# Attention scores in plain fp32 in two row tiles of TensorE, in a hybrid Hyena, Conformer and memory-attention encoder

## The chip, the cores and the metric

The kernel runs on one core of a Trainium2 chip. A core has a matrix engine (TensorE, PE in the profile; its weight loads are PEld), three engines for elementwise work (VectorE or DVE, ScalarE or ACT, GpSimd or POOL), a queue engine (SyncE or SP), and 16 DMA engines. Each engine works through its own instructions in order; they wait for each other through semaphores. TensorE writes its results to PSUM, from where VectorE and ScalarE read them. The metric is the device time of one execution in microseconds (us).

## The reference

Two request groups, each a sequence of 2048 positions with 1024 channels and a memory of 256 tokens, go through the same encoder layer. One projection `h @ w_in` of the normalised input feeds three branches: a Hyena branch (a short convolution, a long convolution by FFT, gates), a Conformer branch (gated, a convolution of 31 taps, LayerNorm), and attention with 4 heads of 64 channels into the memory tokens. The branches are gated, joined, projected by `w_out`, added to the input and normalised. All of it is fp32. What the change touches is this:

```python
def memory_attention(q, mem_n, w_kv):
    k, v = jnp.split(mem_n @ w_kv, 2, axis=-1)
    q = q.reshape(B, L, N_XHEADS, HEAD_DIM)
    k = k.reshape(B, M, N_XHEADS, HEAD_DIM)
    v = v.reshape(B, M, N_XHEADS, HEAD_DIM)
    s = jnp.einsum('blhd,bmhd->bhlm', q, k).astype(jnp.float32) * (HEAD_DIM ** -0.5)
    p = jax.nn.softmax(s, axis=-1).astype(v.dtype)
    o = jnp.einsum('bhlm,bmhd->blhd', p, v)
    return o.reshape(B, L, D_XATTN)
```

## The kernel before

**Stages.** The projection stage normalises x, splits it into a high and a low part (`xh`, `xl`, a type that TensorE multiplies at reduced precision, F32R) and computes 26 columns of 128 channels for each of the two request groups (L426 to L428: high times high, low times high, high times low, over 8 slices of 1024 channels). Each column runs over 4 blocks of 512 tokens; the result of each stands in a PSUM tile `pj` (2 buffers), and a small function for the kind of column reads it out. Between the blocks a background queue is worked off in steps: keys and values of the memory, the Conformer branch, the Hyena filter, the first of the Hyena FFT. The last columns of group 0 are worked together with the loading, normalising and splitting of the next group's x. The attention stage handles 16 blocks of 512 queries of a pair of heads (`attention`), and between them 24 first-stage FFT steps of the Hyena branch (`stage_a`, two to a block as long as there are any; the transposes of L178 and the matmuls of L185 are theirs). The stage after it does the rest of the long convolution (`stage_b`), the last stage the inverse transform, `w_out` and the final norm.

**Order.** The kernel is written in a tile framework that plans the order of each engine's instructions by its own simulation of the time line, and puts in the semaphores. So the order on an engine is not that of the code: the scores of the next half block run ahead of Hyena steps written before them. A tile that is reused waits for its last reader.

**Queries.** `xa_q` scales the projection by 0.125 and splits it: ScalarE writes the high part (L533), VectorE the rest (L534). Both read `pj`. Four DMAs on SP (L537) store the parts to `QS` in DRAM, so that 64 rows hold the high and 64 the low part of a head. `queries` loads a block, 512 KB, on GpSimd's queue (L733), one block ahead.

**Keys.** `kv_background` transposes the keys and writes them four heads wide with the high part in both halves of the partitions and the low part beside zeros (L586 to L589), and stores them to `KB`. `load_kv` loads them for the attention stage (L722).

**Scores.** With high and low parts stacked over the 128 rows, a score tile of 128 queries by 256 memory tokens is two matmuls over all 128 rows (L757): the stacked query parts against the high keys twice over, and against the low keys with zeros. For each half block `u` of 256 queries and each tile `t` of 128, both heads stand in one PSUM tile `sc` (`ms`, 2 buffers). VectorE takes the negated maximum (L761), ScalarE the exponential with its sum (L765), VectorE the reciprocal, GpSimd the product (L769). TensorE transposes the four parts (L772), ScalarE or VectorE copies them out (L774), and after both `t` plain fp32 matmuls multiply them with the values (L779), the two heads in the two halves of the array's columns.

**Places.** The attention stage's SBUF tiles lie where x lay before: `woh[0:4]` under the high x tile of token block 0, `wol[0:4]` under that of block 2. Keys, values and queries use such places, since `w_out` comes into them only later: keys and values of group 0 in `woh[0]`, `woh[1]` and `woh[3]`, those of group 1 in `wol[0:3]`, queries in `woh[2]` and `wol[5]` in turn.

Of the kernel before, what the change touches and what calls it, by code (L numbers as in the profile page):

```python
# [18 lines left out]
P = 128  # L19
L = 2048  # L20
# [82 lines left out]
def kernel(ctx: ExitStack, tc: tile.TileContext, a: dict):  # L103
# [11 lines left out]
    QS = [[dram.tile([2, 64, 2, L], F32R, name=f"qs{g}{c}") for c in range(2)] for g in range(2)]  # L115
    ZX = [[dram.tile([P, L], F32, name=f"zx{g}{c}") for c in range(2)] for g in range(2)]
    KB = [dram.tile([P, 2048], F32R, name=f"kb{g}") for g in range(2)]
# [81 lines left out]
    with ExitStack() as c1:  # L199
# [10 lines left out]
        def sm(n=TB, dt=F32):  # L210
            return smp.tile([P, n], dt, tag="sm", name=nm("sm"))
# [318 lines left out]
        def xa_q(g, i):  # L530
            def f(tb, ps):
                qh, ql = sm(TB, F32R), sm(TB, F32R)
                nc.scalar.activation(qh, ps, AF.Copy, scale=0.125)  # L533
                nc.vector.scalar_tensor_tensor(ql, ps, 0.125, qh.bitcast(F32), op0=ALU.mult, op1=ALU.subtract)  # L534
                for j, q in enumerate((qh, ql)):
                    for h in range(2):
                        nc.sync.dma_start(QS[g][i][j, :, h, tb * TB:(tb + 1) * TB].bitcast(F32),  # L537
                                          q[64 * h:64 * h + 64, :].bitcast(F32))
            return (COL_Q + i * P, f)

        def kv_background():
# [24 lines left out]
            def store(g):  # L566
# [13 lines left out]
                kt = big(2048, F32R)  # L580
                kb = kt.rearrange("p (h q m) -> p h q m", h=4, q=2)
                for h in range(4):
                    r = slice(64 * (h % 2), 64 * (h % 2) + 64)
                    ro = slice(64 - 64 * (h % 2), 128 - 64 * (h % 2))
                    src = pk[r, (h // 2) * 256:(h // 2 + 1) * 256]
                    nc.scalar.copy(kb[r, h, 0, :], src)  # L586
                    nc.scalar.copy(kb[ro, h, 0, :], src)
                    nc.vector.tensor_tensor(kb[0:64, h, 1, :], src, kb[r, h, 0, :].bitcast(F32), op=ALU.subtract)
                    nc.gpsimd.memset(kb[64:128, h, 1, :].bitcast(F32), 0.0)  # L589
                nc.sync.dma_start(KB[g].bitcast(F32), kt.bitcast(F32))  # L590

# [112 lines left out]
    with ExitStack() as c2:  # L704
# [14 lines left out]
        def load_kv(g):  # L719
            kt, vt = ((woh[0:2], woh[3]), (wol[0:2], wol[2]))[g]  # L720
            for i in range(2):
                nc.gpsimd.dma_start(kt[i], KB[g][:, i * 1024:(i + 1) * 1024])  # L722
            vt = vt.bitcast(F32)[:, 0:512]
# [284 lines left out]
```

## Time and profile before

| | |
|---|---|
| median of three runs | 2121.18 us (2119.74 to 2125.28) |
| the profiled execution, its own time | 2124.94 us |
| its span, first to last instruction | 2123.2 us |
| TensorE matmuls busy | 1993.2 us, 94% |
| VectorE, GpSimd, ScalarE busy | 1267.3, 895.0, 758.1 us |

The profile is of one execution. A row of a group gives line, engine, operation, out<-in, the shapes, and how many there are; "idle before" is the time in which the engine stood still in front of it, and what ended that. A matmul's duration holds the time that its results need through the array, so matmuls that follow each other overlap; what one costs in a stream is read from the distance of the starts.

### The profile page before, as it was taken

How to read it: one execution, taken by the hardware profiler on the slowest of the kernel's cores; microseconds unless marked ns; L12 is line 12 of the kernel's file. 1: busy time of each engine (PE TensorE's matmuls, PEld its weight loads, DVE VectorE, ACT ScalarE, POOL GpSimd, SP SyncE). 2: the span in 40 equal slices, each digit the busy share in tenths (PEclk: the TensorE clock that was granted, in tenths of full speed). 3: DMA queues.
4: the chain of work that ended last, by engine and by line, in shares of the span. 5: the costliest groups of instructions: out<-in, count | busy, mean ns of one | idle time of the engine just before them, and what ended most of it. 6: DMA issues, size and time to landing. Idle time of an engine off the chain costs nothing.

```text
span 2123.2 us, 26265 instructions
## 1 busy us (share of the span) xinstructions
PE 1993.2 (94%) x9058; PEld 1552.7 (73%) x9058; DVE 1267.3 (60%) x1747; ACT 758.1 (36%) x1439; POOL 895.0 (42%) x854
## 2 busy tenths in 40 slices
PE   5999988898999999999999899999988899999998
PEld 5888877786877788786777777767433378888886
DVE  5756397978326364469595963278787533444443
ACT  5531212131424233231333244278687611112111
POOL 3423476655533111455554541266598611111111
PEclk9999999999999999999999999999999999999999
DMA  9643333332656422222322236688888685565552
GB/s 337 207 150 134 95 90 100 110 110 79 213 194 219 129 106 100 75 91 81 90 87 107 80 111 207 224 275 264 238 273 271 215 197 153 145 152 145 153 149 55
DMA packets 238557, 329.71 MB, mean 155 GB/s; under 512 B 87177, under 2 KB 117913, under 8 KB 236634
## 3 DMA queue, kind: packets, MB, share of 16 engines
q1 hardware_dynamic: 146026, 261.70, 39.3%
q10 hardware_dynamic: 87056, 54.57, 9.2%
q0 software_dynamic: 5344, 11.77, 2.0%
q8 instruction: 72, 1.18, 0.2%
q14 instruction: 59, 0.48, 0.1%
HBM read 197.35 MB, written 130.61 MB: 154 GB/s over the span
## 4 chain that ended last, share of the span: by engine, by line
PE 58%; DVE 18%; DMA 8%; POOL 6%; issue 5%; ACT 4%; SPq 1%; ACTq 0%; POOLq 0%; DVEq 0%
DVE bg L230 11%; PE pj L427 10%; PE pj L426 10%; PE pj L428 10%; PE ms L953 5%; PE ms L955 5%; PE ms L954 5%; PE tr L936 2%; DMA bg<-in_x_sample_dram 2%; DMA in<-x1d 2%; DVE sm L449 2%; PE tr L772 1%; PE po L779 1%; PE ms L757 1%; PE ms L564 1%
## 5 line engine op out<-in xcount | busy, mean ns | idle before, releaser
L426 PE MATMUL pj<-xh,whi 128*128 128x512 f32 (+1 forms) x1728 | 671.5, 389 | 30.7 <-ACT sm L440 8.4
L427 PE MATMUL pj<-xl,whi 128*128 128x512 f32 (+1 forms) x1728 | 670.2, 388 | 7.4 <-POOL xl L397 5.1
L428 PE MATMUL pj<-xh,wlo 128*128 128x512 f32 (+1 forms) x1728 | 668.8, 387 | 0.3 <-DMA wlo<-ws 0.3
L230 DVE SCALAR_TENSOR_TENSOR bg<-bg,vb,bg 128x512 f32<-128x512 f32 x480 | 419.7, 906 | 12.9 <-POOL bg L225 8.0
L426 PEld LDWEIGHTS pj<-xh,whi 128*128 128x128 f32 x1728 | 331.7, 192 | 101.5 <-ACT sm L440 10.4
L427 PEld LDWEIGHTS pj<-xl,whi 128*128 128x128 f32 x1728 | 332.2, 192 | 72.5 <-POOL xl L397 6.2
L428 PEld LDWEIGHTS pj<-xh,wlo 128*128 128x128 f32 x1728 | 331.9, 192 | 64.9 <-DMA wlo<-ws 0.8
L953 PE MATMUL ms<-wo,mh 128*128 128x512 f32 x512 | 207.0, 404 | 2.0 <-ACT mh L188 2.0
L954 PE MATMUL ms<-wo,mh 128*128 128x512 f32 x512 | 201.5, 394 | 0.0
L955 PE MATMUL ms<-wo,ml 128*128 128x512 f32 x512 | 198.8, 395 | 0.0
L447 POOL TENSOR_SCALAR sm<-sm,va 128x448 f32<-128x448 f32 (+1 forms) x96 | 121.2, 1263 | 159.2 <-ACT sm L440 152.9
L449 DVE SCALAR_TENSOR_TENSOR sm<-sm,va,sm 128x448 f32<-128x448 f32 (+1 forms) x96 | 83.9, 874 | 153.4 <-POOL sm L447 122.8
L956 DVE TENSOR_TENSOR xr<-xr,ms 128x512 f32<-128x512 f32 x64 | 44.0, 687 | 203.4 <-PE ms L955 202.4
L468 POOL TENSOR_TENSOR big<-big,sm 128x448 f32<-128x448 f32 (+1 forms) x64 | 120.2, 1878 | 102.8 <-DVE sm L451 99.4
L195 POOL TENSOR_TENSOR ss<-ss,mhalf 128x1 f32<-128x1 f32 x32 | 17.7, 552 | 315.8 <-DVE ss L194 315.8
L193 ACT ACTIVATE junk<-xr 128x1024 bf16<-128x1024 f32 x32 | 33.8, 1057 | 318.4 <-DVE xr L956 318.4
L440 ACT COPY sm<-pj 128x512 f32<-128x512 f32 x96 | 56.1, 585 | 220.3 <-PE pj L428 186.9
L953 PEld LDWEIGHTS ms<-wo,mh 128*128 128x128 f32 x512 | 97.4, 190 | 20.8 <-ACT mh L188 2.8
L955 PEld LDWEIGHTS ms<-wo,ml 128*128 128x128 f32 x512 | 96.4, 188 | 20.8 <-POOL ml L189 0.3
L954 PEld LDWEIGHTS ms<-wo,mh 128*128 128x128 f32 x512 | 97.4, 190 | 19.2
L189 POOL TENSOR_TENSOR wlo<-sm,whi 128x512 fp32r<-128x512 f32 x50 | 79.7, 1608 | 63.4 <-ACT whi L188 47.3
L827 POOL TENSOR_TENSOR z<-z,us 128x512 f32<-128x512 f32 x64 | 81.5, 1283 | 33.9 <-DVE us L826 26.2
(171 smaller groups left out, 2877.7 us busy)
## 6 DMA issues: line engine op xcount, KB each, us to landing
big<-in_xt_dram SPq DMA_DIRECT2D x32, 512.0 KB, 5.5
in<-x1d SPq DMA_DIRECT2D x128, 128.0 KB, 3.8
aa<-o ACTq DMA_DIRECT2D x64, 256.0 KB, 4.1
at<-aa SPq DMA_DIRECT2D x64, 256.0 KB, 3.9
out_dram<-xr ACTq DMA_DIRECT2D x64, 256.0 KB, 3.4
sm<-in_win_dram SPq DMA_DIRECT2D x52, 256.0 KB, 3.2
ws<-whi SPq DMA_DIRECT2D x52, 256.0 KB, 2.2
ws<-wlo SPq DMA_DIRECT2D x52, 256.0 KB, 4.0
```

Of the source, the lines that this page charges most:

```text
L189: (sub_eng or nc.gpsimd).tensor_tensor(lo, src, hi.bitcast(F32), op=ALU.subtract)
L230: nc.vector.scalar_tensor_tensor(st["a", c], st["h", c][:, k:k + TB], vb[:, 2 * k + c:2 * k + c + 1], st["a", c], op0=ALU.mult, op1=ALU.add)
L426: nc.tensor.matmul(ps[:, ts_], hi, xh[:, k, ts_], start=k == 0, stop=False)
L427: nc.tensor.matmul(ps[:, ts_], hi, xl[:, k, ts_], start=False, stop=False)
L428: nc.tensor.matmul(ps[:, ts_], lo, xh[:, k, ts_], start=False, stop=k == KC - 1)
L447: nc.gpsimd.tensor_scalar(ct[:, o:e], pt[:, o + 1:e + 1], w[1], va[:, 52 + ch:53 + ch], op0=ALU.mult, op1=ALU.add)
L449: nc.vector.scalar_tensor_tensor(ct[:, o:e], pt[:, o:e], w[0], ct[:, o:e], op0=ALU.mult, op1=ALU.add)
L468: nc.gpsimd.tensor_tensor(v, v, out, op=ALU.mult)
L827: nc.gpsimd.tensor_tensor(z, z, us, op=op)
L953: nc.tensor.matmul(po, mh[:, k, :], woh[k][:, hs], start=i == 0, stop=False)
L954: nc.tensor.matmul(po, mh[:, k, :], wol[k][:, hs], start=False, stop=False)
L955: nc.tensor.matmul(po, ml[:, k, :], woh[k][:, hs], start=False, stop=i == 7)
```

## The change

Queries and keys are no longer split. `xa_q` is one ScalarE copy and one store. The keys are stored as they come from the transposes, with the two heads of a pair on rows 0 to 63 and 64 to 127. A score tile is one plain fp32 matmul over 64 rows, and the two heads' matmuls lie in the upper and the lower half of the array's rows (row tiles). They write two PSUM tiles: `sc[h]` holds a head with both `t` side by side, instead of a `t` with both heads. Maximum, exponentials, reciprocal and product are then done for each head, and the transposes of a `t` come after both heads' products. Keys and values of group 0 now lie in `woh[0]` and `woh[1]`, those of group 1 in `woh[2]` and `woh[3]`, and queries in `wol[0]` and `wol[1]` in turn.

```diff
     HD = [[dram.tile([P, L + 2 * CH], F32, name=f"hd{g}{c}") for c in range(2)] for g in range(2)]
     SZ = [[dram.tile([P, L], F32, name=f"sz{g}{c}") for c in range(2)] for g in range(2)]
-    QS = [[dram.tile([2, 64, 2, L], F32R, name=f"qs{g}{c}") for c in range(2)] for g in range(2)]
+    QS = [[dram.tile([P, L], F32, name=f"qs{g}{c}") for c in range(2)] for g in range(2)]
     ZX = [[dram.tile([P, L], F32, name=f"zx{g}{c}") for c in range(2)] for g in range(2)]
-    KB = [dram.tile([P, 2048], F32R, name=f"kb{g}") for g in range(2)]
+    KB = [dram.tile([P, 512], F32, name=f"kb{g}") for g in range(2)]
...
         def xa_q(g, i):
             def f(tb, ps):
-                qh, ql = sm(TB, F32R), sm(TB, F32R)
-                nc.scalar.activation(qh, ps, AF.Copy, scale=0.125)
-                nc.vector.scalar_tensor_tensor(ql, ps, 0.125, qh.bitcast(F32), op0=ALU.mult, op1=ALU.subtract)
-                for j, q in enumerate((qh, ql)):
-                    for h in range(2):
-                        nc.sync.dma_start(QS[g][i][j, :, h, tb * TB:(tb + 1) * TB].bitcast(F32),
-                                          q[64 * h:64 * h + 64, :].bitcast(F32))
+                q = sm()
+                nc.scalar.activation(q, ps, AF.Copy, scale=0.125)
+                nc.sync.dma_start(QS[g][i][:, tb * TB:(tb + 1) * TB], q)
...
                         nc.tensor.transpose(pk[:, i * 256 + s * P:i * 256 + (s + 1) * P],
                                             kv[:, s * 256 + i * P:s * 256 + (i + 1) * P], ident)
-                kt = big(2048, F32R)
-                kb = kt.rearrange("p (h q m) -> p h q m", h=4, q=2)
-                for h in range(4):
-                    r = slice(64 * (h % 2), 64 * (h % 2) + 64)
-                    ro = slice(64 - 64 * (h % 2), 128 - 64 * (h % 2))
-                    src = pk[r, (h // 2) * 256:(h // 2 + 1) * 256]
-                    nc.scalar.copy(kb[r, h, 0, :], src)
-                    nc.scalar.copy(kb[ro, h, 0, :], src)
-                    nc.vector.tensor_tensor(kb[0:64, h, 1, :], src, kb[r, h, 0, :].bitcast(F32), op=ALU.subtract)
-                    nc.gpsimd.memset(kb[64:128, h, 1, :].bitcast(F32), 0.0)
-                nc.sync.dma_start(KB[g].bitcast(F32), kt.bitcast(F32))
+                kt = bt()
+                nc.scalar.copy(kt, pk)
+                nc.sync.dma_start(KB[g], kt)
...
 
         def load_kv(g):
-            kt, vt = ((woh[0:2], woh[3]), (wol[0:2], wol[2]))[g]
-            for i in range(2):
-                nc.gpsimd.dma_start(kt[i], KB[g][:, i * 1024:(i + 1) * 1024])
-            vt = vt.bitcast(F32)[:, 0:512]
+            kt, vt = (t.bitcast(F32)[:, 0:512] for t in (woh[2 * g], woh[2 * g + 1]))
+            nc.gpsimd.dma_start(kt, KB[g])
             nc.gpsimd.dma_start(vt, VT[g])
-            kvs[g] = ([t.rearrange("p (h q m) -> p h q m", h=2, q=2) for t in kt],
-                      vt.rearrange("p (i m c) -> p i m c", i=2, m=2))
+            kvs[g] = (kt.rearrange("p (i m) -> p i m", i=2), vt.rearrange("p (i m c) -> p i m c", i=2, m=2))
 
         qn = [0]
 
         def queries(g, i, tb):
-            qt = (woh[2], wol[5])[qn[0] % 2]
+            qt = wol[qn[0] % 2].bitcast(F32)[:, 0:TB]
             qn[0] += 1
-            nc.gpsimd.dma_start(qt.rearrange("p (h t) -> p h t", h=2),
-                                QS[g][i][:, :, :, tb * TB:(tb + 1) * TB].rearrange("q r h t -> (q r) h t"))
+            nc.gpsimd.dma_start(qt, QS[g][i][:, tb * TB:(tb + 1) * TB])
...
                 pt = pts[pn[0] % 6]
                 pn[0] += 1
+
+                sc = ms(), ms()
                 for t in range(2):
-                    sc = ms()
                     for h in range(2):
-                        q0 = h * TB + u * 256 + t * P
-                        for j in range(2):
-                            nc.tensor.matmul(sc[:, h * 256:(h + 1) * 256], qt[:, q0:q0 + P], kb[i][:, h, j, :],
-                                             start=j == 0, stop=j == 1)
+                        r, q0 = slice(64 * h, 64 * h + 64), u * 256 + t * P
+                        nc.tensor.matmul(sc[h][:, t * 256:(t + 1) * 256], qt[r, q0:q0 + P], kb[r, i, :],
+                                         start=True, stop=True)
+                e = []
+                for h in range(2):
                     mx = tiny.tile([P, 2], F32, tag="mx", name=nm("mx"))
                     se = tiny.tile([P, 2], F32, tag="se", name=nm("se"))
-                    nc.vector.tensor_reduce(mx, sc.rearrange("p (h m) -> p h m", h=2), axis=AX.X, op=ALU.max,
+                    nc.vector.tensor_reduce(mx, sc[h].rearrange("p (t m) -> p t m", t=2), axis=AX.X, op=ALU.max,
                                             negate=True)
-                    e = eps_[2 * u + t]
-                    for h in range(2):
-                        nc.scalar.activation(e[:, h * 256:(h + 1) * 256], sc[:, h * 256:(h + 1) * 256], AF.Exp,
-                                             bias=mx[:, h:h + 1], accum_out=se[:, h:h + 1])
+                    e.append(eps_[2 * u + h])
+                    for t in range(2):
+                        nc.scalar.activation(e[h][:, t * 256:(t + 1) * 256], sc[h][:, t * 256:(t + 1) * 256], AF.Exp,
+                                             bias=mx[:, t:t + 1], accum_out=se[:, t:t + 1])
                     nc.vector.reciprocal(se, se)
-                    ev = e.rearrange("p (h m) -> p h m", h=2)
+                    ev = e[h].rearrange("p (t m) -> p t m", t=2)
                     nc.gpsimd.tensor_tensor(ev, ev, se.unsqueeze(2).broadcast_to([P, 2, 256]), op=ALU.mult)
+                for t in range(2):
                     tp = tr()
                     for k in range(4):
-                        nc.tensor.transpose(tp[:, k * P:(k + 1) * P], e[:, k * P:(k + 1) * P], ident)
-                    tv = tp.rearrange("p (k t) -> p k t", k=4)
-                    (nc.vector.tensor_copy if t else nc.scalar.copy)(pt[:, :, t * P:(t + 1) * P], tv)
+                        nc.tensor.transpose(tp[:, k * P:(k + 1) * P],
+                                            e[k // 2][:, t * 256 + k % 2 * P:t * 256 + (k % 2 + 1) * P], ident)
+                    (nc.vector.tensor_copy if t else nc.scalar.copy)(
+                        pt[:, :, t * P:(t + 1) * P], tp.rearrange("p (k t) -> p k t", k=4))
```

## Rows read from the trace of the kernel before

**Rows 1.** The page: the span, and a group of part 5 (columns as explained above).
```profile
span 2123.2 us, 26265 instructions
...
L426 PE MATMUL pj<-xh,whi 128*128 128x512 f32 (+1 forms) x1728 | 671.5, 389 | 30.7 <-ACT sm L440 8.4
```
**Rows 2.** Busy time by stretch (window, length, busy us of each engine, clock, DMA, GB/s).
```profile
100.00:160.00 60.00, 60.00 (x267) 49.17 (x266) 38.76 (x66) 22.07 (x49) 17.12 (x20) 1.00 0.41 147
```
**Rows 3.** Waits of PE, 594 to 705 us (total us, times, longest).
```profile
PE pj L426 <- DVE sm L534: 5.8, 5, 2.0
```
**Rows 4.** Timeline around one of these waits (start us, length us).
```profile
645.37 0.59 ACT L533 ACTIVATE sm<-pj 128x512 fp32r<-128x512 f32 x1
...
648.95 0.50 PE L426 MATMUL pj<-xh,whi 128*128 128x512 f32 x1 [1.08 <-DVE sm L534]
```
**Rows 5.** Busy time by stretch, attention stage (order PE, PEld, DVE, ACT, POOL).
```profile
1438.00:1458.00 20.00, 20.00 (x157) 14.62 (x154) 15.89 (x33) 16.61 (x54) 13.43 (x17) 1.00 0.91 288
```
**Rows 6.** Timeline of PE over one block of the attention stage.
```profile
1443.73 1.20 PE L757 MATMUL ms<-wo,wo 128*128 128x256 f32 x8
...
1448.20 1.20 PE L757 MATMUL ms<-wo,wo 128*128 128x256 f32 x8
1449.24 0.60 PE L178 MATMUL tr<-ident,u 128*128 128x128 f32 x4
1449.77 1.08 PE L779 MATMUL po<-ynp,wo 128*64 128x256 f32 x8
1450.79 0.66 PE L772 MATMUL tr<-ident,ynp 128*128 128x128 f32 x4
1451.38 0.50 PE L185 MATMUL pa<-k,th 64*128 64x512 f32 x2
1451.71 0.40 PE L185 MATMUL pa<-k,tl 64*128 64x512 f32 x2
1451.95 0.39 PE L185 MATMUL pa<-k,th 64*128 64x512 f32 x2
1452.27 0.66 PE L772 MATMUL tr<-ident,ynp 128*128 128x128 f32 x4
1452.68 1.20 PE L757 MATMUL ms<-wo,wo 128*128 128x256 f32 x8
1453.81 0.51 PE L185 MATMUL pa<-k,th 64*128 64x512 f32 x2
```
**Rows 7.** Timeline of GpSimd's queue at the end of the projection stage.
```profile
1354.57 0.73 POOL L733 DMA_DIRECT2D wo<-qs  x1
...
1363.73 1.08 POOL L722 DMA_DIRECT2D wo<-kb  x2 [4.72 <-PE pj L428]
```
**Rows 8.** The query loads of L733, all 16: from issue to landing.
```profile
DMA to landing us min/median/max: 4.2/5.7/9.2
```
**Rows 9.** Timeline at the start of the attention stage.
```profile
1368.70 0.63 PE L757 MATMUL ms<-wo,wo 128*128 128x256 f32 x4
...
1370.14 0.68 DVE L761 TENSOR_REDUCE mx<-ms 128x2 f32<-128x512 f32 x1
...
1370.85 0.47 ACT L765 ACTIVATE ynp<-ms,mx 128x256 f32<-128x256 f32 x1
```
**Rows 10.** Three lines' matmuls (records, ns min/median/max, first and last start).
```profile
L757 PE MATMUL ms<-wo,wo x256: 274/283/682, 1368.7 to 1514.1; 128*128 128x256 f32 x128
...
L820 PE MATMUL tr<-in,stab x128: 592/592/1061, 1505.5 to 1685.2; 128*128 128x512 f32 x128
...
L779 PE MATMUL po<-ynp,wo x256: 379/379/431, 1380.7 to 1524.5; 128*64 128x256 f32 x128
```
**Rows 11.** Timeline of ACT: the last accumulator read of a half block.
```profile
1451.94 0.22 ACT L765 ACTIVATION_READ_ACCUMULATOR ynp<-ms,mx 128x1 f32 x1
```
**Rows 12.** Timeline of PE where no Hyena step is left.
```profile
1496.92 1.08 PE L779 MATMUL po<-ynp,wo 128*64 128x256 f32 x8
...
1500.65 1.08 PE L779 MATMUL po<-ynp,wo 128*64 128x256 f32 x8
```

## The prediction

> **What bounds the kernel now.** I read the page first, then the busy times by stage, then for each stage the waits of TensorE and the timeline. The profiled execution spans 2123.2 us [rows 1]. The change touches three places: the query and key steps of the projection stage (0 to 1368 us), the start of the attention stage (1368 to 1378 us), and the attention stage itself (to about 1526 us).
>
> In the projection stage TensorE is nearly always busy; where the keys are stored (137 to 149 us) it is busy in every microsecond [rows 2]. So work on ScalarE, VectorE and GpSimd counts here only where TensorE waits for it. The list of waits has one such place: in the last chunks of the first request group, TensorE waits five times, 5.8 us together, for the subtraction of L534 [rows 3]. One of the five shows why: ScalarE has read the projection out by 645.96 us (645.37 + 0.59), but the PSUM tile comes free only after VectorE, which is deep in the normalisation of the second group, has done its half as well; the next projection starts at 648.95 us, 1.08 us late [rows 4].
>
> In the attention stage TensorE is busy 20.00 of 20 us, the other engines at most 17 [rows 5]. TensorE's timeline there is a row of groups without gaps; the score group that stands in front of L185 returns from 1443.73 to 1452.68 us, so a block takes 8.95 us and half a block (256 queries, one score group) 4.48 us [rows 6]. What this stage is worth is therefore read from TensorE's order of groups, and from whether a new wait enters it.
>
> **The change, part by part.**
>
> *Queries.* It removes 16 subtractions on VectorE and 48 of 64 stores on SP. Ten of the subtractions hide behind TensorE and are worth nothing, the last belongs to the start of the attention stage below, and the five above are worth at most 5.8 us. With ScalarE alone reading, the tile of rows 4 is free 2.25 us before TensorE is. Behind the wait I find nothing that comes due at once except the casts of the next x tiles, which follow TensorE on ScalarE's queue and so move with it. I take 5.0 us of gain, bounds 0 (the order of the stage's instructions is planned anew, and another wait takes the place) and 5.8.
>
> *Keys.* 16 casts, 8 subtractions and 8 memsets become 2 copies. All lie under the full 60 us of TensorE in rows 2: nothing, and were the cover gone, a gain.
>
> *Start of attention.* The first queries go from a place that lay under the x tile of the first token block to one under the third block's (the two are freed in the order in which the last projections end). Before, the load was issued at 1354.57 us; now it can't be before about 1363.73 us, where the second group's keys, which lay under that same tile, got their release [rows 7]. GpSimd's queue behind it (second queries, second keys, the first u block) waited for that release in any case. Landing takes 4.2 to 9.2 us, median 5.7 [rows 8], so the queries are there at 1369.4 us (1367.9 to 1372.9), against first scores at 1368.70. But the first exponential starts only at 1370.85 us [rows 9]; scores from 1369.4, a group of 1.1 us (below) and a reduction of 0.68 [rows 9] make 1371.2. The last subtraction, which held up the first reduction until 1370.14, is gone, but the exponential waits no longer for that than for the scores. I take +0.5 us, bounds -0.5 and +3.
>
> *Score matmuls.* First the streaming. A split matmul of 512 columns takes 389 ns [rows 1], one of 256 columns 283 [rows 10]: 106 ns per 256 columns. Plain fp32 shows two records per matmul (L779: 256 for 128 calls), 592 ns at 512 columns and 379 at 256 [rows 10]: 213 ns per 256 columns and record, 427 per matmul. Per half block the old scores are 8 records; their row spans 1.04 us to the next transposes [rows 6], of which I take off 0.08 that still lies under the transposes ahead (a row of four of these spans 0.41 us and lasts 0.66): 0.96. The new ones are 4 matmuls, 8 records of 213 ns in two row tiles. The trace of before has no plain fp32 in row tiles, so bounds: with no overlap 8 x 0.213 = 1.70 us; with full overlap 0.85. Two rows lie near: plain fp32 in two column tiles gives 8 records in 1.02 us, and the split matmuls of 64 rows in L185 give pairs 0.24 us apart, where two of them one after the other would stream for 0.43 [rows 6]. Both overlap, so I take 4 slots of 0.226 (between 0.213 and 0.24), 0.90 us: 0.06 less than before.
>
> *Switching.* Groups in tiles cost something at both ends. Four transposes take 0.41 us in front of a full-array group and 0.53 in front of a tiled one; the step from the last pair of L185 to the transposes is 0.32 where pairs are 0.24 apart; the first pair after the entry takes 0.33; and four transposes behind a tiled group last 0.66 us against 0.60 [rows 6]. That is 0.12 + 0.09 + 0.08 + 0.06, about 0.36 us a visit. The old scores were full-array and paid none. A new score group that stands alone costs 0.36 - 0.06 = +0.30; one next to L185 shares its visit: -0.06. In the order of before one group of each block stands directly in front of L185 (1452.68, then 1453.81) and one between transposes (1448.20) [rows 6]. With that order, the 12 blocks that still have hyena work between (of 16) give 12 x 0.30 - 12 x 0.06 = +2.9 us; bounds -1.4 (all next to a tiled group) and +7.2 (all alone).
> The Trainium skill's page TensorEngine Tiling (Array Packing), Key Properties, says that changing the tiling mode, as against only the tile, drains TensorE. It speaks against this change; the trace agrees in kind (0.53 against 0.41), and what it would cost if every group paid it is a rival below.
>
> *Order of the softmax.* Before, each of a half block's two score tiles needs one bank, and the first reduction can start when half the group is done. Now both banks are written to the group's end, the first reduction starts about 0.45 us later, and the next group needs both banks free, so it waits for all four pairs of exponential and accumulator read. Before, from score start (1448.20) to the end of the last accumulator read (1452.16) [rows 6, 11] it is 3.96 us, and the next group starts 0.52 later. Now 3.96 + 0.45 = 4.41 in a half block of 4.48 plus the 0.12 added above: it just fits. Behind a late score group on TensorE's queue stand the transposes, the second product and L185. In the steady blocks I take nothing, bounds 0 and +0.3 a half block. In the two blocks where no hyena work is left to fill, a half block takes 3.73 us (1496.92 to 1500.65) [rows 12], and the longer chain shows: 4 x 0.4 = +1.6 us, bounds 0 and +4 (the last two blocks too).
>
> *Transposes.* The same count, of both heads together; the copies and everything after keep count and shape. Query loads halve, 4.2 MB of the stage's traffic; TensorE waits for no transfer there, so nothing.
>
> **Sum.** -5.0 + 0.5 + 2.9 + 0 + 1.6 = 0.0 us on 2124.94 us, the profiled execution's own time (span 2123.2 and 1.7 around it). That execution lies 3.8 us over the median of the runs, 2121.18, so the median forecast is 2121. What a measurement of this kernel tells from no change is about 0.3%, 6.4 us.
>
> **Rivals.**
> *Forecast: gain and loss cancel*, 2121 (2115 to 2127). For it: rows 3 is a real wait of TensorE; by rows 5 and 6 TensorE pays for each switch.
> *Faster, 2114:* the five waits go wholly (-5.8) and the planner sets all score groups next to tiled ones (-1.4), start and tail nothing: -7.2. For it: half of them stand so already. Against: the new scores become ready at another time than the old.
> *Each group pays its switch:* all 32 groups alone, 32 x 0.30 = 9.6; -5.0 + 0.5 + 9.6 + 1.6 = +6.7, 2128. For it: a group now becomes ready when the second bank is free, at a time that no L185 shares. It decides against the forecast from some 30 lone groups on. The rule of the Trainium skill's page TensorEngine Tiling (Array Packing) above, taken alone, leads here.
> *The wait for both banks binds:* place, TensorE's queue in front of each score group; price, what the chain of 4.41 us exceeds the half block by. From 0.2 us more on ScalarE or VectorE in that chain it decides: 0.3 us over in 24 half blocks is +7.2, 2128; 0.5 is +12, 2133. For it: 0.52 us of slack, and ScalarE and VectorE over 70% busy [rows 5]. Against: a planner that sees the wait can move other work in front.
> *The row tiles don't overlap in plain fp32* (the change doesn't do what it says): 0.85 us more per group, 32 x 0.85 = +27, 2148. Against: both near rows overlap.
>
> **Chances and range.** Forecast 0.48, faster 0.17, lone groups 0.13, both banks 0.13, no overlap 0.09. The middle one's spread leaks 0.02 to faster; of the two slower rivals near 2128 some 0.04 falls within 0.3%. That makes faster 0.19, same 0.50, slower 0.31. The range from 2112 to 2134 takes in four of the five and leaves out the last, and the far end of the both-banks wait. The forecast's own range is 2115 to 2127.
>
> **What would show it.** In the profile after: no wait of TensorE for the query step at 594 to 705 us, and the attention stage starting some 5 us earlier; pairs of score records within some 10 ns of each other, pairs 0.22 us apart; a score group of about 0.9 us and 0.1 us more idle on TensorE around it; blocks of about 9.2 us; VectorE's first reduction after the group's end. Wrong if: score records follow each other singly by 0.213 us (no overlap); TensorE waits for ScalarE's exponentials in front of scores for more than some 3 us in all (both banks); the projection stage is as long as before, or longer, with waits elsewhere (the planner).

## The result, and the profile after

The change makes the kernel slower: 2159.33 us median of four runs (2156.11 to 2163.02) against 2120.46 (2118.81 to 2125.28), a ratio of 1.0181 with a 95% interval of 1.0166 to 1.0197. The forecast was 2121, with a range to 2134. The profiled execution took 2160.55 us, its span is 35.6 us longer than that of [rows 1]. Columns are as in [rows 1].

```profile
span 2158.8 us, 26096 instructions
...
L426 PE MATMUL pj<-xh,whi 128*128 128x512 f32 (+1 forms) x1728 | 674.3, 391 | 38.2 <-ACT xh L396 9.5
...
L428 PE MATMUL pj<-xh,wlo 128*128 128x512 f32 (+1 forms) x1728 | 671.4, 389 | 6.1 <-POOL wlo L189 6.1
```

The 35.6 us are three parts, read from the starts of three kinds of record. The last projection matmul starts at 1384.52 us instead of 1368.47: +16.0. From the first score to the last matmul of the second product it is 180.4 us instead of 155.8: +24.6. From there to the first matmul of the last stage it is 175.2 instead of 180.3: -5.1.

**The projection stage.** Waits of TensorE from 150 to 720 us (total us, times, longest):

```profile
PE pj L426 <- DMA whi<-ws: 9.3, 2, 6.7
...
PE pj L428 <- POOL wlo L189: 6.1, 1, 6.1
PE pj L426 <- ACT sm L533: 2.7, 2, 1.6
```

The five waits of [rows 3] are gone, as forecast. Two of them, 2.7 us, are left in another form: TensorE now waits for the query step's own ScalarE copy (L533). And two long ones are new. The first is at 178 us (timeline: start, length, what it waited for):

```profile
162.55 23.09 POOL L189 TENSOR_TENSOR wlo<-sm,whi 128x512 fp32r<-128x512 f32 x2 [10.27 <-ACT whi L188]
176.77 9.41 DVE L230 SCALAR_TENSOR_TENSOR bg<-bg,vb,bg 128x512 f32<-128x512 f32 x11
...
182.86 1.63 DVE L230 SCALAR_TENSOR_TENSOR bg<-bg,vb,bg 128x512 f32<-128x512 f32 x1
183.91 1.73 POOL L189 TENSOR_TENSOR wlo<-sm,whi 128x512 fp32r<-128x512 f32 x1
184.00 0.79 PE L428 MATMUL pj<-xh,wlo 128*128 128x512 f32 x1 [6.11 <-POOL wlo L189]
```

GpSimd computes the low part of the next column's weights. It has its input at 162.55 us, and the first of its two subtractions ends only at 183.95, while VectorE works through a row of convolution taps (L230). Until 182.83 us these taps overlap: each takes 0.75 us, and the next starts 0.66 us after it. At 182.83 there is a gap of 0.04 us between two of them for the first time. The tap behind the gap takes 1.63 us, and within that time GpSimd's subtraction ends. The second subtraction then takes 1.73 us, though the taps go on. How long these subtractions last in each kernel up to 600 us (ns min/median/max), first before, then after:

```profile
L189 POOL TENSOR_TENSOR wlo<-sm,whi x44: 1271/1488/7100, 11.6 to 589.3; 128x512 fp32r<-128x512 f32 x44
```
```profile
L189 POOL TENSOR_TENSOR wlo<-sm,whi x44: 1272/1312/21402, 11.6 to 597.6; 128x512 fp32r<-128x512 f32 x44
```

The same subtraction takes 1.3 us or 21.4. Before, its worst case was 7.1, and TensorE did not wait for it. The Trainium skill's page SBUF — State Buffer, section SBUF: two separate sides, says that VectorE and GpSimd share a pair of ports as an exclusive lock, held for a whole instruction, when VectorE has two SBUF inputs and GpSimd reads SBUF. The trace agrees: L230 reads two tiles, L189 reads SBUF, and in the gap GpSimd takes over and holds VectorE up. It shows in addition that GpSimd got no turn for 20 us, as long as the taps overlapped. Behind the wait, the clock is down (windows after the change; columns as [rows 2]): 1.2 GHz from 184 to 188 us, after TensorE had stood for 6 us, with 9 matmuls in 4 us where 18 fit at 2.4 GHz.

```profile
178.00:184.00 6.00, 0.00 (x0) 0.00 (x0) 5.96 (x9) 0.14 (x1) 6.00 (x2) 0.78 0.00 0
184.00:188.00 4.00, 4.00 (x9) 3.14 (x10) 3.86 (x5) 0.00 (x0) 1.64 (x1) 0.50 0.55 208
```

The second wait is at 704 us, in the timeline of SP's queue and of TensorE:

```profile
701.32 3.92 DVE L397 TENSOR_TENSOR xl<-big,xh 128x1024 fp32r<-128x1024 f32 x2
...
704.17 0.81 SPq L367 DMA_DIRECT2D big<-in_xt_dram  x2
705.07 0.38 SPq L415 DMA_DIRECT2D whi<-ws  x1
...
711.04 0.80 PE L426 MATMUL pj<-xh,whi 128*128 128x512 f32 x1 [6.75 <-DMA whi<-ws]
```

SP works in order. The load of an x tile (L367) had stood at its head since 696.2 us and waited for VectorE's subtraction (L397) to free the buffer. Behind it stood the load of the next column's weights (L415), which went out as soon as the queue moved. Before, the weight loads went out from 689.3 to 697.0 us among the x loads, none of which waited for L397 longer than 2.2 us (from 640 to 712 us).

**The attention stage.** TensorE's timeline in one block, to be held against [rows 6]:

```profile
1461.41 1.13 PE L741 MATMUL ms<-wo,wo 64*128 64x256 f32 x4 [0.16 <-ACT ynp L751]
1462.31 0.53 PE L185 MATMUL pa<-k,th 64*128 64x512 f32 x2
...
1463.24 0.66 PE L759 MATMUL tr<-ident,ynp 128*128 128x128 f32 x4
1463.82 1.13 PE L741 MATMUL ms<-wo,wo 64*128 64x256 f32 x4
1464.88 1.08 PE L767 MATMUL po<-ynp,wo 128*64 128x256 f32 x8
1465.89 0.66 PE L178 MATMUL tr<-ident,u 128*128 128x128 f32 x4
1466.48 1.13 PE L741 MATMUL ms<-wo,wo 64*128 64x256 f32 x4
1467.54 0.66 PE L178 MATMUL tr<-ident,u 128*128 128x128 f32 x4
...
1469.73 0.70 PE L741 MATMUL ms<-wo,wo 64*128 64x256 f32 x2
1470.06 0.50 PE L185 MATMUL pa<-k,th 64*128 64x512 f32 x1
1470.27 0.38 PE L741 MATMUL ms<-wo,wo 64*128 64x256 f32 x1
```

A half block should show one score group of 8 records. Instead there are groups of 4, one head each, far apart. In such a group the records follow each other by 0.216 us, one at a time, and the whole takes 1.06 us to the next work, as long as a group of both heads would. Only some 60 of the 256 score records lie within 50 ns of another. TensorE never waits in this stretch for more than 0.2 us; it is busy, with half of the array's rows idle. The steady blocks take 9.44 and 11.72 us in turn, 10.58 in the mean, against 8.95. (A block is measured here from VectorE's product of one block to that of the next.)

### The profile page after: what moved, and what is told of

Its sections match the earlier page's. It is cut to its first block, busy times and chain, and to the rows that moved or that the text cites. A ratio compares the mean times of both kernels' runs of the same rounds, so it can differ in the third digit from the quotient of the medians.

```text
span 2158.8 us, 26096 instructions
## 1 busy us (share of the span) xinstructions
PE 2019.8 (94%) x9058; PEld 1562.1 (72%) x9058; DVE 1254.7 (58%) x1723; ACT 755.5 (35%) x1427; POOL 899.2 (42%) x844
## 4 chain that ended last, share of the span: by engine, by line
PE 60%; DVE 16%; DMA 10%; POOL 5%; issue 5%; ACT 3%; SPq 1%; ACTq 0%; POOLq 0%; DVEq 0%
DVE bg L230 10%; PE pj L428 10%; PE pj L427 10%; PE pj L426 10%; PE ms L941 5%; PE ms L943 5%; PE ms L942 5%; PE tr L924 2%; PE ms L741 2%; DMA bg<-in_x_sample_dram 2%; DMA in<-x1d 2%; POOL wlo L189 2%; DVE sm L449 1%; PE po L767 1%; PE tr L759 1%
## 5 line engine op out<-in xcount | busy, mean ns | idle before, releaser
L230 DVE SCALAR_TENSOR_TENSOR bg<-bg,vb,bg 128x512 f32<-128x512 f32 x480 | 415.1, 902 | 11.2 <-POOL bg L225 7.1
L189 POOL TENSOR_TENSOR wlo<-sm,whi 128x512 fp32r<-128x512 f32 x50 | 93.3, 1878 | 63.4 <-ACT whi L188 47.3
L377 DVE SCALAR_TENSOR_TENSOR big<-big,va,ms 128x256 f32<-128x256 f32 x144 | 58.2, 476 | 55.9 <-PE ms L375 40.7
```

Source lines behind the costliest of these rows:

```text
L189: (sub_eng or nc.gpsimd).tensor_tensor(lo, src, hi.bitcast(F32), op=ALU.subtract)
L230: nc.vector.scalar_tensor_tensor(st["a", c], st["h", c][:, k:k + TB], vb[:, 2 * k + c:2 * k + c + 1], st["a", c], op0=ALU.mult, op1=ALU.add)
L377: nc.vector.scalar_tensor_tensor(xb[:, k, :], xb[:, k, :], va[:, g0 + k:g0 + k + 1], r, op0=ALU.mult, op1=ALU.mult)
```

## The experiments

The first four split the loss by place and by cause.

**1. Scores kept together.** The kernel after, with the four score matmuls of a half block chained.

```diff
+                last = None
                 for t in range(2):
-                    for h in range(2):
+                    for h in (1, 0):
...
-                        nc.tensor.matmul(sc[h][...], qt[r, q0:q0 + P], kb[r, i, :], start=True, stop=True)
+                        with (tc.issue_after(last) if last else ExitStack()):
+                            last = nc.tensor.matmul(sc[h][...], qt[r, q0:q0 + P], kb[r, i, :], ...).ins
```

> The kernel after, but each half block's four score matmuls are told to follow one another directly on TensorE (upper and lower half of the rows in turn). In the trace of after only 58 of 256 score records lie within some 15 ns of another; most run in groups of 4 records of one head. Theory A (heads issued apart: no overlap, and a tiled visit more per half block): records come in pairs again, a steady block falls from a mean of 10.58 us to about 9.2, the attention stage (first score to last second product) from 180.4 to about 160, the total from 2159 to about 2137; the projection stage stays 16 us longer than before. Rival B (the chain through both banks and the softmax by head sets the block): the pairs come back, but a wait in front of the scores takes their place; the block stays over 10 us, the total over 2150. Rival C (plain fp32 is dearer in itself, by its two records per matmul): less than 5 us change.

Measured: 2145.02 us (ratio 1.0107, 1.0082 to 1.0132), 14 less than after; 214 of 256 records in pairs, steady block 9.32, attention stage 162.0 us. TensorE's timeline:

```profile
1464.79 0.66 PE L761 MATMUL tr<-ident,ynp 128*128 128x128 f32 x4
1465.37 1.14 PE L743 MATMUL ms<-wo,wo 64*128 64x256 f32 x8
1466.44 0.66 PE L761 MATMUL tr<-ident,ynp 128*128 128x128 f32 x4
...
1469.43 0.60 PE L761 MATMUL tr<-ident,ynp 128*128 128x128 f32 x4
1469.96 1.14 PE L743 MATMUL ms<-wo,wo 64*128 64x256 f32 x8
1470.74 0.59 PE L185 MATMUL pa<-k,th 64*128 64x512 f32 x2
```

All 8 records now take 1.07 us where 4 took 1.06, and 0.78 where L185 follows. Theory A holds in size: of the 24.6 us, 18.4 are gone. Only the order was changed, so the order is what these 18.4 us come from; the lost overlap and the additional tiled visits went together and aren't separated by this run. The total came out 8 above its figure; in this execution the projection stage was another 5 us longer. With unchanged order that stage's end varied from 1365.0 to 1371.7 us over five other profiles below, so single differences of 3 us in it are not read.

**2. The old projection stage under the new attention.** `xa_q`, `kv_background` and the stores as before; attention as after, its loads taking the high parts:

```diff
...
-            nc.gpsimd.dma_start(qt, QS[g][i][:, tb * TB:(tb + 1) * TB])
+            for h in range(2):
+                nc.gpsimd.dma_start(qt[64 * h:64 * h + 64, :], QS[g][i][0, :, h, tb * TB:(tb + 1) * TB]...)
```

> The projection stage of the kernel before (queries and keys split and stored as there, the same planned order of instructions), with the attention stage of after, which loads only the high parts; the low parts of queries and keys are left out of the scores. If the 16 us of the projection stage come from the edits of the query and key steps (new order on the engines, with new waits of TensorE), the last projection matmul starts at about 1368.5 us again, and the total is about 2143; the attention stage keeps its 180 us. If they come from something else (the clock in that execution, another place of the buffers), the stage keeps some 1384 us and the total about 2159.

Measured: 2145.68 us (1.0116, 1.0094 to 1.0137). The last projection matmul starts at 1371.65, the attention stage takes 180.0 us. The projection loss comes from the edits of the query and key steps.

**3. The new projection stage under the old attention.**

```diff
...
-            nc.gpsimd.dma_start(qt.rearrange(...), QS[g][i][:, :, :, tb * TB:(tb + 1) * TB]...)
+            nc.gpsimd.dma_start(qt.bitcast(F32).rearrange("p (h t) -> p h t", h=2),
+                                QS[g][i][:, tb * TB:(tb + 1) * TB].unsqueeze(1).broadcast_to([P, 2, TB]))
```

> The reverse: the projection stage of after, with the attention stage of before (full-array split scores, softmax by tile), whose operands are loaded twice over from the unsplit stores, so that the scores are not the reference's. If the two costs are independent, the projection stage ends at about 1384.5 us, the attention stage takes about 156 us again, and the total is about 2138 (2120 + 16, with the two to three us that the longer last stretch may give or take). If the time is set by the attention stage alone, about 2121.

Measured: 2138.63 us (1.0086, 1.0062 to 1.0109); projection to 1385.6, attention 155.2. Within the intervals the two losses add up: 0.86% here and 1.16% in run 2 make 2.0%, against 1.81% (1.66 to 1.97).

**4. The order of the softmax alone.**

```diff
+                sc = ms(), ms()
...
-                    sc = ms()
...
-                            nc.tensor.matmul(sc[:, h * 256:(h + 1) * 256], qt[:, q0:q0 + P], kb[i][:, h, j, :], ...)
+                            nc.tensor.matmul(sc[h][:, t * 256:(t + 1) * 256], qt[:, q0:q0 + P], kb[i][:, h, j, :], ...)
```

> Before, with its split full-array matmuls, but with a PSUM tile for each head instead of for each 128 queries: maximum, exponentials, reciprocal and product by head, and the transposes after both. No row tiles, no plain fp32 in the scores. Theory A: only what both banks cost, block 8.95 to 9.3 us, total 2120 to 2127. Rival B (the order of the softmax, and the wait for both banks, is what lengthens the block): the block comes to over 10 us, the total to over 2135.

Measured: 2123.35 us (1.0010, 0.9996 to 1.0024). In the total, maximum, exponentials and product by head cost nothing that can be measured, as long as the planner may move work in front of a score group that waits. The attention stage itself did grow, from 155.8 to 159.7 us. The blocks are no longer steady, 7.4 to 11.2 us; the first 11 intervals take 102.99 us instead of 100.43, and the last one 18.5 instead of 14.9. The stretch from there to the last stage is 6.3 us shorter.

**5 and 6. Which edit costs the projection stage what.** Before with the new query step alone, and with the new key step alone (the diffs are those of the change).

> Before, with the new query step alone (one ScalarE copy, one store); keys as before, attention of before on operands loaded twice over, so the scores are not the reference's. If the query step does what the forecast said, its five waits of TensorE go and the projection stage ends 4 to 6 us earlier than before, total 2114 to 2118. If the query step brings the 16 us (its new place in the plan gives the wait of 6.75 us at 704 us), the stage ends later by 6 to 16 us, total 2127 to 2137.

> Before, with the new key step alone (one copy, one store for each request group); queries as before, and the attention of before on keys loaded twice over, so the scores are not the reference's. The forecast said nothing for it (under full TensorE): 2121. If the key step re-orders the background work behind it, so that TensorE waits 6.1 us at 178 us for the low weight part from GpSimd, the stage ends 6 to 16 us later: 2127 to 2137.

Measured: queries 2129.07 us (1.0035, 1.0020 to 1.0050), keys 2128.11 (1.0033, 1.0016 to 1.0050). Start of the n-th projection record against that in the profile of before, in us:

```
record            400    700   2400   2600   2700   last
after            -2.1   +6.4   +8.1   +6.8  +13.0  +16.0
queries alone    +0.6   +0.7   +0.6   -0.7   +3.9   +3.9
keys alone       -0.6   +7.6   +9.4  +10.0   +9.6   +6.9
run 9            -0.9   -0.8   -1.6   -3.0   -3.5   +2.3
```

The keys bring the wait at 178 us (8.2 us with the low clock). The queries first gain: 1.3 us from record 2400 to 2600, where two of the five waits were (1.8 us). Then SP's queue takes 4.6: two waits for weights of 2.1 and 5.3 us and the low clock behind the second (0.50 for 4 us), less the other three waits of before, which are gone. Against the expectations, both totals lie in the second range, but the stage ends only 3.9 us later with the queries, not 6 to 16. The record numbers must not be read too finely: the norms' matmuls of the next x stand between the records, at other places in each run.

**7. Both undone**, the old projection stage and the paired scores (edits of 1 and 2 together).

> Both undone: the projection stage of before (queries and keys split and stored; the low parts are left out of the scores), and the attention of after with the four score matmuls of a half block told to follow one another, heads in turn. If the two costs are independent: last projection matmul near 1370, steady blocks 9.32 us as in the run with the pairs alone, total 2145.7 - 14 to 18 = 2128 to 2132, less what the last stretch gives. If the forecast's terms for the attention stage (+2.9 for the visits, +1.6 for the tail) are right by themselves, 2122 to 2128. Over 2135 neither holds.

Measured: 2136.47 us (1.0073, 1.0049 to 1.0097), above both figures, so neither holds; projection to 1366.5, but blocks of 10.00 us, not 9.32. The timeline shows why:

```profile
1456.69 1.13 PE L759 MATMUL ms<-wo,wo 64*128 64x256 f32 x8
1457.47 0.58 PE L185 MATMUL pa<-k,th 64*128 64x512 f32 x1
1457.89 0.39 PE L185 MATMUL pa<-k,tl 64*128 64x512 f32 x1
1458.12 0.39 PE L185 MATMUL pa<-k,th 64*128 64x512 f32 x1
1458.44 0.66 PE L777 MATMUL tr<-ident,ynp 128*128 128x128 f32 x4
1459.03 0.50 PE L185 MATMUL pa<-k,th 64*128 64x512 f32 x1
...
1459.92 0.87 PE L785 MATMUL po<-ynp,wo 128*64 128x256 f32 x6
```

L185 is in row tiles too, and here its two halves are apart: twice three records, 0.97 and 0.89 us, instead of six in 0.90. The same loss at another place, in another plan; run 10 tests it.

**8. Heads in turn.** Run 7 with the loops over `t` and `h` exchanged, so that both matmuls of head 1 stand before both of head 0.

> As the run with the old projection stage and the pairs, but head 1's two matmuls first and then head 0's, still all four in a row: the same count of tiled visits, the overlap of the row tiles lost but for the place where the heads meet. Records of a half block then stand 0.216 us apart one by one. Price of the lost overlap alone: 3 to 4 slots of 0.216 in 32 half blocks, 21 to 28 us over that run; near nothing if the hardware overlaps the two heads whatever their order.

Measured: 2132.97 us (1.0056, 1.0036 to 1.0076), blocks of 10.01. The guess of 21 to 28 us was wrong, the other half of the expectation right: the group still takes 1.07 us, and its records still start in pairs, 13 ns apart.

```profile
1409.06 1.14 PE L759 MATMUL ms<-wo,wo 64*128 64x256 f32 x8
1410.13 0.44 PE L777 MATMUL tr<-ident,ynp 128*128 128x128 f32 x2
```

So the order within the group doesn't matter; what matters is that no other work stands between the heads.

**9. The two projection waits mended**, in the kernel after (`late` is the last weight load in front; given only for the last half of the second group's x):

```diff
-                    split(hi, lo, raw, sub_eng=nc.vector if first and h else None)
+                    split(hi, lo, raw, sub_eng=nc.vector if first and h or col == COL_ZC + P else None)
...
+            with (tc.issue_after(late) if late else ExitStack()): 
                 for k in range(0, KC, 4):
                     nc.sync.dma_start(xb[:, k:k + 4, :], src[:, k:k + 4, :])
```

> The kernel after with two edits in the projection stage, attention as in after. (1) The low part of the weights of the column awaited at 178 us is subtracted on VectorE instead of GpSimd, where it had taken 21.4 us beside VectorE's unbroken row of convolution taps. (2) On the DMA queue SP, the last x tile load of the second request group is placed behind the next column's weight loads instead of in front of them; in after it held the queue for 7.9 us, waiting for VectorE, and the weights came 6.7 us late. Theory: the waits of 6.1 and 6.75 us go, with the low clock behind each; the last projection matmul comes 13 to 16 us earlier than in after (1384.5), at about 1369 to 1372, the total at 2143 to 2147. If the waits only move on to another place, under 5 us are gained. If the forecast's gain on the queries (5 us) is real behind them, the stage ends at 1364 to 1367.

Measured: 2145.56 us (1.0118, 1.0102 to 1.0134), last projection matmul at 1370.83, 13.7 us earlier than in after. Both waits are gone, by the table above at their places; the subtraction took 0.68 us on VectorE. Waits of TensorE from 150 to 720 us:

```profile
PE pj L430 <- ACT big L516: 3.1, 1, 3.1
PE pj L430 <- ACT sm L537: 2.8, 2, 1.9
PE pj L430 <- DMA whi<-ws: 2.3, 1, 2.3
```

With the mend the queries' gain shows as 1.9 us from record 2400 to 2700, which holds four of the five waits (4.9 us); two waits for the query step's own copy, 2.8 us, have come in their place. A new wait of 3.1 us (for a sigmoid on ScalarE) follows, and the stage ends 2.3 us later than before, within the scatter named under 1.

**10 and 11. Pairs kept together in both places**: L185 chained like the scores, once on run 7 and once, with the scores, on run 9.

```diff
-            for s in range(2):
+            for s in (1, 0):
...
+                with (tc.issue_after(last) if last else ExitStack()):
+                    last = nc.tensor.matmul(px[s], w[r, :], u[r, :], start=j == 0, stop=j == 2).ins
```

> The run with the old projection stage and paired scores had steady blocks of 10.00 us, not 9.32, and in its trace the six matmuls of L185, which are row tiles too, stand in two groups of three that take 0.97 and 0.89 us instead of one of 0.90 (19 us of the 22 by which 12 blocks would differ come from there and from one more visit). Here L185's six are told to follow one another as well. If the separation of a pair costs wherever it happens: block about 9.3, total 7 to 8 us below that run's 2136, 2128 to 2130. If L185's order is not it: block stays at 10.0.

> The mended projection stage of the run above with scores and L185 both told to stay together in the attention stage. From the parts: 2159 - 14 (projection) - 18 (attention) = 2127, 2122 to 2131. If the two mends are not independent, over 2135.

(The bracket in the first of these is miscounted: twelve blocks that differ by 0.67 us are 8 us, not 22.) Measured: 2132.58 us (1.0058, 1.0042 to 1.0075) and 2134.08 (1.0063, 1.0046 to 1.0080). The blocks fell from 10.00 to 9.33 as expected, and are 9.21 to 9.51 in run 11; both totals lie a few us above their figures. In the total, run 10 can't be told from run 7 (the intervals overlap); that L185's order matters is read from the blocks. Even with every loss found taken away, the new kernel isn't faster than the old one: run 11 is 0.63% slower, and where this remainder comes from was not settled.

**12 and 13. The order written out by hand.** On run 11, one Hyena step to a half block: L185 issued behind the scores, the transposes behind L185, then the second product (12); or the second product of the half block before directly behind L185 and then the transposes (13). `sl` is the last score matmul, `rl` the last of L185, in 13 that of the second product.

```diff
+                with (tc.issue_after(sl[0])):
+                    rl[0] = nc.tensor.matmul(px[s], w[r, :], u[r, :], ...).ins
...
+                    with (tc.issue_after(rl[0])):
                         nc.tensor.transpose(tp[:, k * P:(k + 1) * P], e[k // 2][...], ident)
```

> As the run above, but the attention stage is written out so that in every half block the four paired scores stand directly in front of L185's six matmuls, one hyena step to a half block, and the transposes come behind them: both tiled operations share a visit. Theory (a lone score group pays about 0.3 us for its visit, one next to a tiled group nothing): half block 4.3 to 4.4 us, block 8.6 to 8.8 against 8.95 before, attention stage 150 to 156, total 2114 to 2121. Rival (the chain through both banks, about 4.4 us from score start to the last accumulator read, sets the half block): block 8.9 to 9.2, total 2121 to 2126.

> As the run with the scores in front of L185, but the second product of the half block before stands directly behind L185, and the transposes come after it: scores, L185 and second product share one visit, and VectorE's copies of the transposes have a half block's time to land. There the second product had waited 22 times, 12.6 us in all, for these copies (blocks of 10.15 us). Theory (that wait was the new bound; a shared visit is cheaper than three): half block 4.3 to 4.4, block 8.6 to 8.85, total 2116 to 2124 with the mended projection stage, which ends 2 to 6 us later than before's. Rival (the chain through both score banks comes next): wait of TensorE for the exponentials in front of the scores, block 8.95 or more, total 2125 or more.

Measured: 2147.08 us (1.0132, 1.0111 to 1.0153) with blocks of 10.15, outside both figures, and 2183.98 (1.0297, 1.0272 to 1.0321) with blocks of 12.4 to 14.6. The waits of TensorE in the stage, first of 12, then of 13:

```profile
PE po L781 <- DVE ynp L776: 12.6, 22, 1.9
PE ms L743 <- ACT ynp L754: 3.0, 4, 1.8
```
```profile
PE ms L743 <- ACT ynp L754: 34.7, 39, 2.5
```

In 12 the second product comes too close behind the transposes that it needs. With that taken away, 13 runs into the wait for both score banks, of 0.7 us or more in front of 25 of the 32 score groups: the rival expected there, and more than it said. Whether shared visits would be cheaper could not be seen under these waits.

## Why the prediction was wrong

The sum was 0.0, the profile says +35.6. By its steps:

*Score matmuls* is the step that failed first. "Both overlap, so I take 4 slots of 0.226" was right about the chip: 0.216 us per pair, when the heads stand together (run 1). It took for granted that they do. In before both heads of 128 queries share a PSUM tile, and none of their matmuls needs a partner; after, each head has its own tile, and the planner put other work between the heads. That the tiles come free at different times is the likely reason, not a shown one. The rival "row tiles don't overlap", 2148, named this price but not this reason; the hardware overlaps them, the order didn't. It cost 18 of the 24.6 us.

*Switching* (+2.9) fits in size once the groups are whole: over the first 11 intervals between blocks, run 1 is 2.6 us longer than before (103.06 against 100.43); after is 14.8 longer. But run 4, whose scores are in no row tiles, is as long (102.99). So that the 2.6 us are the price of switching isn't shown; the agreement may be luck. A price of switching does show where the rows allow it to be read: a score group takes 1.07 us by itself and 0.78 where L185, tiled too, follows (run 1).
The Trainium skill's page TensorEngine Tiling (Array Packing), Key Properties, says that a change of tiling mode drains TensorE. The trace agrees in kind, by the 0.29 us just named. In a lone head's group of 1.06 us, though, the four records' 0.216 us each, 0.86 in all, are the larger part: what a parted pair costs is mostly its lost overlap.

*Keys* (0) failed. The window of [rows 2] was read for TensorE where the keys are stored; the loss came 30 us later. Before, the eight key subtractions on VectorE stood between the taps, and the taps overlapped for 14 us (158.9 to 173.2 us); without them they did so for 30 (152.3 to 182.8; in run 6, with the new keys alone, 153.8 to 184.3), over a subtraction on GpSimd that had its input at 162.55. "Were the cover gone, a gain" left out that a shorter step moves what follows it. 8.2 us of 16.

*Queries* (-5.0). The five waits went, but no gain is left at the end of the stage (runs 5 and 9): other waits took their place, 2.7 us of them in after for the query step's own ScalarE copy, which the prediction had taken to be free in time. (Its 2.25 us for that are 1.9: by [rows 4] TensorE was free at 647.87 us.) "Behind the wait I find nothing that comes due at once" had looked at ScalarE's queue and not at SP's, where 48 of 64 stores were taken out and the planner then put a load that waits in front of one that TensorE needed. Its bound of 0, "planned anew", was no bound: a new plan can cost.

*Start* (+0.5): the first score starts 0.32 us after the last projection matmul, before 0.23; nothing lost. *Order of the softmax* (0) was right for the total by run 4 (+0.10%, -0.04 to +0.24), not for the stage, which grew by 3.9 us there. The wait for both banks didn't bind: TensorE waited for exponentials in front of the scores for 3.7 us in all after and for 3.0 before. Without the planner's freedom, in run 13, it did bind. *Tail* (+1.6): the last interval grew by 4.5 us (14.91 to 19.4); 3.6 of these show in run 4 as well, so the softmax by head brings them, as argued, but at more than twice the size. By the last second product 32 records of the next stage were done instead of 26, 15.1 us of TensorE instead of 11.8, so some of the 4.5 may have come back in the -5.1. But in run 4 that stretch is 6.3 us shorter with only 28 records done (12.1 us), so what shortens it stays open.

Why the planner put the two heads, and SP's loads, as it did stays open: its own costs and due times don't show in a trace. That its orders cause the loss is shown by run 1, which changed nothing else, by the blocks of run 10, and by run 9, which also moved one subtraction to VectorE. That the plan might be the trouble stood in the prediction as its last sign of being wrong (a projection stage as long as before or longer, with waits elsewhere), but with no price.

## What to carry to other kernels

Two matmuls that are to share the array must stand next to each other in the order of TensorE, and it pays to tie them together by hand when they write different tiles; a planner can part them, as here, and the profile then shows a busy engine and hardly a wait. In a kernel whose order is planned, an edit that takes work off engines with spare time isn't free: look at which in-order queue the removed instructions stood in, and what now stands behind a waiting one there. Compare the start of the n-th record of a long row of equal work between two profiles: it shows where a loss arises. And a size that comes out as forecast isn't yet the cause that was forecast: run 4 had the 2.6 us without any row tiles in its scores.

## What was not expected of the hardware

Two row tiles overlapped in plain fp32 whatever the order in which their matmuls stood in a group (1.07 us for 8 records in runs 1 and 8, pairs 7 and 13 ns apart), so each half seems to work off its own matmuls. A GpSimd subtraction of 1.3 us took 21.4 us beside VectorE's row of two-input instructions: not one turn in 20 us while these overlapped, and its turn in the first gap between two of them, of 0.04 us, whereupon the VectorE instruction took 1.63 us instead of 0.75. A wait of 6.1 us of TensorE cost 8.2, since the granted clock stood at 0.50 for 4 us behind it.
